# A two-layer decoder trunk on one core: affine halves behind the projection's low weights, the attention scale in the queries, later gate transposes, four up weights on the first token half

## The chip, the cores and the metric

One core of one Trainium2 chip runs the whole program in one launch. The metric is the device time of that launch in microseconds (us); the runs shown are three timed runs and one profiled execution of the kernel before.

## What is computed

The reference is a decoder trunk of two layers over 512 tokens of width 1024, in float32. Cut to what matters here, one layer is:

```python
proj = h @ w_in[l]                      # cq, ckv, kr, xp, xqk, xv, xo, ipre, fpre
a = mla(...)      # q = rms_norm(cq) @ w_uq ; k, v from ckv ; 4 heads, 128 + 64 (rotary)
                  # scale = (128 + 64) ** -0.5
                  # p = softmax(((q_nope * scale) . k_nope + (q_pe * scale) . k_pe) masked)
p = multiscale_pool(xp, ...)
m = mlstm(xqk, xv, xo, ipre, fpre, ...)  # gates give log weights, chunkwise matrix memory
h = layer_norm(ALPHA * h + concat(a, p, m) @ w_out[l])
x, g = split(h @ w_up[l])                # 2 x 2816 columns
h = layer_norm(ALPHA * h + (silu(dwconv(g)) * x) @ w_down[l])
```

A layer norm ends in an affine step, times a gain, plus a bias.

## The kernel before

Every float32 product is made of three products of shorter numbers: each operand x is split into `hi = round(x)` and `lo = x - hi`, and `hi*hi`, `hi*lo` and `lo*hi` are added in PSUM. For weights, `fetch` (L142) does this: SP loads 128x1024 floats into a `raw` buffer (two of them, `raw_...`), ACT casts them to `hi_...` (L158), and DVE, or for a few POOL, subtracts to get `lo_...` (L159). There are four `hi` and four `lo` buffers, used in turn, so a weight can be prepared only when the one four places before it has been used. The names of the weights: `ia`, `it`, `ib` (input projection), `uq`, `uk`, `uv`, `o{half}_{q}` (output projection, two halves of 512 columns, four chunks of 256 rows each; a trace row calls all of them `lo_o`), `up` and `d` (the MLP).

**Order of the work.** PE's instructions stand in the order in which a small planner in the program, `Order`, emits them: generators yield a cost, a delay, or the name of an event that they wait for, and the planner moves its own clock by them. The other engines' instructions are put in order by a scheduler from priorities and estimates when the program is built. Each engine runs its own list strictly in order; what it needs from another engine it waits for.

**Gates.** `mlstm` (L575 on) takes the forget gates to four rows of 512, makes two scans over them on DVE, and exponentiates the row `mr` on ACT (L597). After a delay of 10.0 in the planner (L598), PE turns `lf_r` and `mr` into columns by eight small transpositions into `cols` (L601, L602). Then come `mq` and `mk`, two block-diagonal products for each half j of the convolved channels `c[j]` (L616), and later the scores `st`. Between these, PE works on the input projection's chunks `ib`.

**Attention.** `att_scores` (L770 on) makes a block of scores `s_`, takes its row maximum `mx` on DVE (L791), multiplies it by -SCALE (L792), and ACT forms `exp(SCALE*s + mx)` with its row sum `sm` (L795). DVE takes the reciprocal (L796) and multiplies (L797); PE transposes the result (`pt`, L814).

**Output projection and norm.** `out_gen(0)` and `out_gen(1)` make the two halves. `h` is the residual stream, reloaded from the DRAM tile `spill` in four tiles of 128 tokens (L894); it was stored without its affine step, so `pre_affine(i, half)` multiplies 128x512 of it by the gain (L898) and adds the bias (L899), both on DVE. Then `resid` adds the product (L842) and takes statistics (L193). For `half == 0`, each `resid` also emits `pre_affine(i, 1)`, the affine step of the other half. In the second half, all tokens pass chunk 0 first; then, per token tile i, chunks 1, 2 and 3. `ln_tail` finishes a tile's norm: aggregate (L202), `rs` (L189, and a power on POOL, L190), normalise (L217). PE then transposes the tile (`tp_a`, L228) for the up projection.

**Up projection.** `t_half` makes its first products with 256 tokens (token tiles 0 and 1) for three weights, `up_0_0`, `up_0_1` and `up_1_0`, and then again for tiles 2 and 3 (L325); `t_one` makes the others with all 512 (L173 to L175).

Of the kernel before, what the change touches and what calls it, by code (L numbers as in the profile page):

```python
# [10 lines left out]
F32 = mybir.dt.float32  # L11
F32R = mybir.dt.float32r
BF16 = mybir.dt.bfloat16
AF = mybir.ActivationFunctionType
# [6 lines left out]
NT = S // P  # L21
# [74 lines left out]
def trunk(ctx: ExitStack, tc: tile.TileContext, I: dict, out: bass.AP, layers=DEPTH):  # L96
# [41 lines left out]
    wloaded = []  # L138
    first_raw = []

    def add_w(src, n, name, eng, rows=1):
        wlist.append((src, n, name, eng, rows))  # L142

    def fetch():
        src, n, name, eng, rows = wlist[len(wloaded)]
        if len(wloaded) < len(first_raw):
            raw = first_raw[len(wloaded)][:, :n]
        else:
            raw = stream.tile([P, CH], F32, tag="raw", bufs=2, name="raw_" + name)[:, :n]
        nc.sync.dma_start(raw, src)  # L150
        hi = stream.tile([P, CH], F32R, tag="whi", bufs=4, name="hi_" + name)
        lo = stream.tile([P, CH], F32R, tag="wlo", bufs=4, name="lo_" + name)
        if rows == 1:
            h_, l_, r_ = hi[:, :n], lo[:, :n], raw
        else:
            h_, l_ = [t.rearrange("p (r c) -> p r c", r=rows)[:, :, : n // rows] for t in (hi, lo)]
            r_ = raw.rearrange("p (r c) -> p r c", r=rows)
        A.copy(h_, r_)  # L158
        eng.tensor_tensor(l_, r_, h_.bitcast(F32), ALU.subtract)  # L159
        wloaded.append((hi, lo, name))  # L160
# [281 lines left out]
    for l in range(layers):  # L442
# [130 lines left out]
        def mlstm():  # L573
# [23 lines left out]
            A.activation(mr, mr, AF.Exp, scale=-1.0)  # L597
            yield 0.6, 10.0, None  # L598
            cols = bank("cols")
# [134 lines left out]
        def q_handler(base):  # L734
            def f(m, o):
                t = base + m
                if t < 4:
                    qn[t] = t4r(f"qn{t}")
                    split(*qn[t], o)
                    sch.set(f"qn{l}_{t}", 1.79)  # L740
# [32 lines left out]
        def att_scores():  # L773
            for hd in range(H):
# [4 lines left out]
                for qt in range(NT):  # L779
# [10 lines left out]
                    mx = small.tile([P, 1], F32, tag="mx", bufs=4, name="mx")  # L790
                    V.reduce_max(mx, s_[:, :n], AX.X)  # L791
                    V.tensor_single_scalar(mx, mx, -SCALE, ALU.mult)  # L792
                    p = pr[:, roff[qt] : roff[qt] + n]
                    sm = small.tile([P, 1], F32, tag="sm", bufs=4, name="sm")
                    A.activation(p, s_[:, :n], AF.Exp, bias=mx[:, 0:1], scale=SCALE, accum_out=sm)  # L795
                    V.reciprocal(sm, sm)  # L796
# [36 lines left out]
        def resid(which, nm, half, stt, cols=None, tail=True, dst=None):  # L833
            def f(i, ps):
# [4 lines left out]
                with ExitStack() as hs:  # L839
# [3 lines left out]
                    ln_stats(h, i, half, stt[i])  # L843
                if half == 0 and which == "g1":
                    hbox["pre"](i, 1)
                if half == 1:
# [61 lines left out]
        def ffn_open():  # L908
# [3 lines left out]
            fbox["lo"] = fa.tile([P, NF, S], F32R, name="f_lo")  # L912

        hold = {}
        f_sub = [None]
# [19 lines left out]
        def ffn_main():  # L935
            yield from until(o0)
            yield from until(out_gen(1))
            ffn_open()
            hbox["g1"] = load_gb(hp, I["ln1_g"][l], I["ln1_b"][l], "1")
            for k in range(NT):  # L940
                sch.add(ln_affine(h, k, hbox["g1"], f"f{l}_{2 + 2 * k}", lambda: f_sub[0]), 0)
            w1 = [[f"hT_a{l}_{i}" for i in range(2 * hf, 2 * hf + 2)] for hf in range(2)]
            yield from consume(t_half([f"up{l}_0_0", f"up{l}_0_1", f"up{l}_1_0"], w1),
                               lambda n, o: up_consume(n // 2, n % 2, o))
            for n in range(3, 2 * NF):
                yield from consume(t_one(f"up{l}_{n // 2}_{n % 2}"), lambda _, o, n=n: up_consume(n // 2, n % 2, o))
# [78 lines left out]
def tables():  # L1025
    inv = (1.0 / (np.float32(10000.0) ** (np.arange(0, ROPE, 2, dtype=np.float32) / np.float32(ROPE)))).astype(np.float32)
    ang = (np.arange(S, dtype=np.float32)[:, None] * inv[None, :]).astype(np.float32)
    cos, sin = np.cos(ang).astype(np.float32).T, np.sin(ang).astype(np.float32).T
    cs = np.zeros((P, 2, S), np.float32)
    for b in range(0, P, 64):  # L1030
        cs[b : b + 32, 0], cs[b + 32 : b + 64, 0] = cos, cos
        cs[b : b + 32, 1], cs[b + 32 : b + 64, 1] = sin, -sin
    icnt = np.zeros((P, 2, 16), np.float32)
# [24 lines left out]
```

## Time and profile before

| | |
|---|---|
| three timed runs | 1177.37, 1179.7, 1181.1 us (median 1179.7) |
| the profiled execution | 1175.83 us |
| its span, first to last instruction | 1174.0 us |
| mean granted clock of TensorE | 0.992 of full speed |
| PE busy | 1142.0 us, 97% of the span |
| DVE busy | 626.9 us, 53% |
| ACT busy | 469.0 us, 40% |
| POOL busy | 225.3 us, 19% |

PE is busy nearly all the time, so the time of the program is the work on PE plus the stretches in which PE waits or runs at the lower of its two clocks. The sum of a prediction is made against the profiled execution's own 1175.83 us.

### The profile page before, as it was taken

How to read it: one execution, taken by the hardware profiler on the slowest of the kernel's cores; microseconds unless marked ns; L12 is line 12 of the kernel's file. 1: busy time of each engine (PE TensorE's matmuls, PEld its weight loads, DVE VectorE, ACT ScalarE, POOL GpSimd, SP SyncE). 2: the span in 40 equal slices, each digit the busy share in tenths (PEclk: the TensorE clock that was granted, in tenths of full speed). 3: DMA queues.
4: the chain of work that ended last, by engine and by line, in shares of the span. 5: the costliest groups of instructions: out<-in, count | busy, mean ns of one | idle time of the engine just before them, and what ended most of it. 6: DMA issues, size and time to landing. Idle time of an engine off the chain costs nothing. (4 is left out here: it accounts for less than half of the span.)

```text
span 1174.0 us, 14137 instructions
## 1 busy us (share of the span) xinstructions
PE 1142.0 (97%) x5447; PEld 948.4 (81%) x5447; DVE 626.9 (53%) x1007; ACT 469.0 (40%) x814; POOL 225.3 (19%) x186
## 2 busy tenths in 40 slices
PE   8999999899999999999999999989999999999997
PEld 5878777788888888888886887868888888888885
DVE  6776986744453343223368569666544443432426
ACT  6573552553333333212266545417433433332110
POOL 0316400015331111000003362000333211110001
PEclk9999999999999999999999999989999999999999
DMA  8331213332332233233343212142333433233321
GB/s 293 104 117 48 85 37 143 127 107 90 105 128 97 101 91 107 90 93 105 102 138 125 64 48 92 45 171 73 115 102 103 130 93 105 90 99 99 91 89 72
DMA packets 34931, 120.77 MB, mean 103 GB/s; under 512 B 4392, under 2 KB 4904, under 8 KB 34864
## 3 DMA queue, kind: packets, MB, share of 16 engines
q1 hardware_dynamic: 34720, 119.61, 31.1%
q8 instruction: 43, 0.70, 0.2%
q10 hardware_dynamic: 144, 0.26, 0.1%
q14 instruction: 24, 0.20, 0.1%
HBM read 113.55 MB, written 6.31 MB: 102 GB/s over the span
## 5 line engine op out<-in xcount | busy, mean ns | idle before, releaser
L173 PE MATMUL t_up<-a_hi,hi_up 128*128 128x512 f32 x656 | 255.2, 389 | 0.0
L174 PE MATMUL t_up<-a_lo,hi_up 128*128 128x512 f32 x656 | 255.2, 389 | 0.0
L175 PE MATMUL t_up<-a_hi,lo_up 128*128 128x512 f32 x656 | 255.2, 389 | 0.0
L159 DVE TENSOR_TENSOR lo_up<-raw_up,hi_up 128x1024 fp32r<-128x1024 f32 x88 | 120.6, 1371 | 154.4 <-ACT hi_up L158 151.3
L158 ACT CAST hi_up<-raw_up 128x1024 fp32r<-128x1024 f32 x88 | 92.7, 1054 | 193.5 <-PE t_up L174 164.1
L930 POOL TENSOR_TENSOR f_lo<-y,f_hi 128x512 fp32r<-128x512 f32 x44 | 77.3, 1757 | 366.7 <-ACT f_hi L929 351.5
L173 PEld LDWEIGHTS t_up<-a_hi,hi_up 128*128 128x128 f32 x656 | 123.1, 188 | 25.6
L175 PEld LDWEIGHTS t_up<-a_hi,lo_up 128*128 128x128 f32 x656 | 123.1, 188 | 25.5
L174 PEld LDWEIGHTS t_up<-a_lo,hi_up 128*128 128x128 f32 x656 | 123.1, 188 | 25.5
L159 DVE TENSOR_TENSOR lo_d<-raw_d,hi_d 128x1024 fp32r<-128x1024 f32 x44 | 53.9, 1224 | 159.6 <-ACT hi_d L158 159.2
L290 PE MATMUL d<-hi_d,f_hi 128*128 128x512 f32 x352 | 137.1, 389 | 0.0
L292 PE MATMUL d<-hi_d,f_lo 128*128 128x512 f32 x352 | 136.9, 389 | 0.0
L291 PE MATMUL d<-lo_d,f_hi 128*128 128x512 f32 x352 | 136.9, 389 | 0.0
L158 ACT CAST hi_d<-raw_d 128x1024 fp32r<-128x1024 f32 x44 | 46.4, 1055 | 176.2 <-PE d L292 157.1
L292 PEld LDWEIGHTS d<-hi_d,f_lo 128*128 128x128 f32 x352 | 66.1, 188 | 13.8
L290 PEld LDWEIGHTS d<-hi_d,f_hi 128*128 128x128 f32 x352 | 66.1, 188 | 13.6
L291 PEld LDWEIGHTS d<-lo_d,f_hi 128*128 128x128 f32 x352 | 66.1, 188 | 13.6
L928 DVE TENSOR_TENSOR y<-y,t_up 128x512 f32<-128x512 f32 x44 | 30.3, 688 | 75.2 <-PE t_up L175 67.4
L923 DVE SCALAR_TENSOR_TENSOR y<-t_up,pp,y 128x511 f32<-128x511 f32 x88 | 65.7, 746 | 8.9 <-ACT y L921 7.3
L924 ACT ACTIVATE y<-y 128x512 f32<-128x512 f32 x44 | 27.8, 632 | 98.2 <-DVE y L923 98.0
L291 PE MATMUL o<-lo_o,a_hi 128*128 128x512 f32 x128 | 51.8, 405 | 8.6 <-DVE lo_o L159 8.6
L190 POOL TENSOR_TENSOR rs_d<-rs_d,nhalf 128x1 f32<-128x1 f32 x8 | 7.7, 968 | 234.9 <-DVE rs_d L189 234.9
(273 smaller groups left out, 1959.6 us busy)
## 6 DMA issues: line engine op xcount, KB each, us to landing
raw_up<-in_w_up_dram SPq DMA_DIRECT2D x88, 512.0 KB, 3.5
raw_d<-in_w_dn_dram SPq DMA_DIRECT2D x44, 512.0 KB, 3.5
raw_o<-in_w_out_dram SPq DMA_DIRECT2D x16, 512.0 KB, 3.5
raw_it<-in_w_it_dram SPq DMA_DIRECT2D x12, 512.0 KB, 3.5
spill<-h SPq DMA_DIRECT2D x8, 512.0 KB, 2.8
raw_ib<-in_w_ib_dram SPq DMA_DIRECT2D x8, 512.0 KB, 3.5
h<-spill SPq DMA_DIRECT2D x8, 512.0 KB, 7.9
raw_uq<-in_w_uq_dram SPq DMA_DIRECT2D x6, 384.0 KB, 2.9
```

The lines of the kernel that those rows point to most:

```text
L158: A.copy(h_, r_)
L159: eng.tensor_tensor(l_, r_, h_.bitcast(F32), ALU.subtract)
L173: T.matmul(o, whi, xhi, start=start, stop=False)
L174: T.matmul(o, whi, xlo, start=False, stop=False)
L175: T.matmul(o, wlo, xhi, start=False, stop=stop)
L290: T.matmul(o, xhi, whi, start=at == 0, stop=False)
L291: T.matmul(o, xhi, wlo, start=False, stop=False)
L292: T.matmul(o, xlo, whi, start=False, stop=at == nk - 1)
L923: V.scalar_tensor_tensor(y[:, t:], o[:, : S - t], w(2 - t), y[:, t:], ALU.mult, ALU.add)
L924: A.activation(y, y, AF.Silu)
L928: V.tensor_mul(y, y, o)
L930: f_sub[0] = G.tensor_sub(fbox["lo"][:, f, :], y, fbox["hi"][:, f, :].bitcast(F32)).ins
```

## The change

1. The affine steps of the second halves are no longer emitted by `resid`. `ffn_main` now emits them one by one during the second half's last group, with an order that puts each behind the subtraction that makes `lo_o1_3`, the projection's last low weight.
2. SCALE is folded into the queries (`qn` by a scaled copy and one scalar_tensor_tensor; the rotary part by scaled tables), so the multiplication of `mx` goes, and `reduce_max` gives the negated maximum.
3. The planner's delay ahead of the gate transposes is 13.0 in place of 10.0.
4. `t_half` takes four up weights on the first token half in place of three.

```diff
+    lo_ins = {}
...
-        eng.tensor_tensor(l_, r_, h_.bitcast(F32), ALU.subtract)
+        lo_ins[name] = eng.tensor_tensor(l_, r_, h_.bitcast(F32), ALU.subtract).ins
...
             A.activation(mr, mr, AF.Exp, scale=-1.0)
-            yield 0.6, 10.0, None
+            yield 0.6, 13.0, None
...
-                    split(*qn[t], o)
+                    A.mul(qn[t][0], o, SCALE)
+                    V.scalar_tensor_tensor(qn[t][1], o, SCALE, qn[t][0].bitcast(F32), ALU.mult, ALU.subtract)
...
-                    V.reduce_max(mx, s_[:, :n], AX.X)
-                    V.tensor_single_scalar(mx, mx, -SCALE, ALU.mult)
+                    V.reduce_max(mx, s_[:, :n], AX.X, negate=True)
...
-                    A.activation(p, s_[:, :n], AF.Exp, bias=mx[:, 0:1], scale=SCALE, accum_out=sm)
+                    A.activation(p, s_[:, :n], AF.Exp, bias=mx[:, 0:1], accum_out=sm)
...
-                if half == 0 and which == "g1":
-                    hbox["pre"](i, 1)
...
+        pre_left = list(range(NT))
...
             yield from until(o0)
-            yield from until(out_gen(1))
+            for y in out_gen(1):
+                if y[0] == "grp":
+                    last_grp = y[1] > 0
+                    continue
+                yield y
+                if last_grp and y[0] > 0 and pre_left:
+                    with tc.issue_after(lo_ins[f"o{l}_1_3"]):
+                        hbox["pre"](pre_left.pop(0), 1)
...
-            yield from consume(t_half([f"up{l}_0_0", f"up{l}_0_1", f"up{l}_1_0"], w1),
+            yield from consume(t_half([f"up{l}_0_0", f"up{l}_0_1", f"up{l}_1_0", f"up{l}_1_1"], w1),
                                lambda n, o: up_consume(n // 2, n % 2, o))
-            for n in range(3, 2 * NF):
+            for n in range(4, 2 * NF):
...
+    qcos, qsin = cos * np.float32(SCALE), sin * np.float32(SCALE)
     for b in range(0, P, 64):
-        cs[b : b + 32, 0], cs[b + 32 : b + 64, 0] = cos, cos
-        cs[b : b + 32, 1], cs[b + 32 : b + 64, 1] = sin, -sin
+        cs[b : b + 32, 0], cs[b + 32 : b + 64, 0] = qcos, qcos
+        cs[b : b + 32, 1], cs[b + 32 : b + 64, 1] = qsin, -qsin
```

The diff does not tell where the instructions come to stand. Three places follow, each from the list of one engine. First DVE of the kernel before, from the last affine steps to the normalisation of token tile 0 (`gb_p` holds gain and bias, `o_0` is the projection of tile 0, `st_a`, `mv_a` and `rs_a` its statistics):

```order
L899 TENSOR_TENSOR h_1967<-h_1967,gb_p 128x512
L842 SCALAR_TENSOR_TENSOR h_1967<-h_1967,o_3_1718 128x512
L898 TENSOR_TENSOR h_1967<-h_1967,gb_p 128x512
L193 BN_STATS st_a_2028<-h_1967 128x6
L899 TENSOR_TENSOR h_1967<-h_1967,gb_p 128x512
L159 TENSOR_TENSOR lo_o_1_2_2070<-raw_o_1_2_2067,hi_o_1_2_2069 128x1024
L159 TENSOR_TENSOR lo_o_1_3_2076<-raw_o_1_3_2073,hi_o_1_3_2075 128x1024
L842 SCALAR_TENSOR_TENSOR h_1967<-h_1967,o_0_2033 128x512
L193 BN_STATS st_a_1995<-h_1967 128x6
L202 BN_AGGR mv_a_2105<-st_a_1995 128x2
L189 TENSOR_SCALAR rs_a_2106<-mv_a_2105 128x1
L217 TENSOR_SCALAR h_1967<-h_1967,mv_a_2105,rs_a_2106 128x1024
```

All sixteen affine instructions, with four residual additions and four statistics, stand ahead of both low weights; behind them only tile 0's own five instructions lead to its normalisation.

DVE of the changed kernel, the same stretch: the low weight `lo_o_1_2` now stands behind two affine instructions.

```order
L160 TENSOR_TENSOR lo_o_1_1_2016<-raw_o_1_1_2013,hi_o_1_1_2015 128x1024
L897 TENSOR_TENSOR h_1951<-h_1951,gb_p 128x512
L898 TENSOR_TENSOR h_1951<-h_1951,gb_p 128x512
L160 TENSOR_TENSOR lo_o_1_2_2046<-raw_o_1_2_2043,hi_o_1_2_2045 128x1024
L897 TENSOR_TENSOR h_1951<-h_1951,gb_p 128x512
L843 SCALAR_TENSOR_TENSOR h_1951<-h_1951,o_0_1703 128x512
```

After it come the other first-half instructions (six affine, four residual, three statistics), then `lo_o_1_3`, one statistic, and this:

```order
L160 TENSOR_TENSOR lo_up_0_0_2058<-raw_up_0_0_2055,hi_up_0_0_2057 128x1024
L897 TENSOR_TENSOR h_1951<-h_1951,gb_p 128x512 x2
L898 TENSOR_TENSOR h_1951<-h_1951,gb_p 128x512 x2
L843 SCALAR_TENSOR_TENSOR h_1951<-h_1951,o_0_2009 128x512
L897 TENSOR_TENSOR h_1951<-h_1951,gb_p 128x512
L194 BN_STATS st_a_1979<-h_1951 128x6
L898 TENSOR_TENSOR h_1951<-h_1951,gb_p 128x512
L203 BN_AGGR mv_a_2087<-st_a_1979 128x2
L897 TENSOR_TENSOR h_1951<-h_1951,gb_p 128x512
L190 TENSOR_SCALAR rs_a_2088<-mv_a_2087 128x1
L898 TENSOR_TENSOR h_1951<-h_1951,gb_p 128x512
L218 TENSOR_SCALAR h_1951<-h_1951,mv_a_2087,rs_a_2088 128x1024
```

The eight affine instructions of the second halves now stand ahead of tile 0's normalisation, four of them in between its own steps.

PE at the gate transposes, before:

```order
L292 MATMUL ib_634<-hi_ib_0_594,a_lo 128x512
L601 MATMUL cols<-ident,lf_r 128x4
L602 MATMUL cols<-ident,mr 128x4
L601 MATMUL cols<-ident,lf_r 128x4
L602 MATMUL cols<-ident,mr 128x4
L601 MATMUL cols<-ident,lf_r 128x4
L602 MATMUL cols<-ident,mr 128x4
L601 MATMUL cols<-ident,lf_r 128x4
L602 MATMUL cols<-ident,mr 128x4
L616 MATMUL mq<-c,wbd 128x512
L616 MATMUL mk<-c,wbd 128x512
L290 MATMUL ib_631<-hi_ib_1_637,a_hi 128x512
```

And in the changed kernel:

```order
L293 MATMUL ib_632<-hi_ib_1_637,a_lo 128x512
L602 MATMUL cols<-ident,lf_r 128x4
L603 MATMUL cols<-ident,mr 128x4
L602 MATMUL cols<-ident,lf_r 128x4
L603 MATMUL cols<-ident,mr 128x4
L602 MATMUL cols<-ident,lf_r 128x4
L603 MATMUL cols<-ident,mr 128x4
L602 MATMUL cols<-ident,lf_r 128x4
L603 MATMUL cols<-ident,mr 128x4
L617 MATMUL mq<-c,wbd 128x512
L617 MATMUL mk<-c,wbd 128x512
L617 MATMUL mq<-c,wbd 128x512
```

The first twelve products of chunk `ib_1` now stand ahead of the transposes, and both pairs of `mq` and `mk` follow them at once; before, six `ib` products stood between the pairs. On PE there is one more move: `up_1_1` is made of 48 products of 256 columns in place of 24 of 512. The transposes of token tile 3 stay where they were, behind 36 of the 256-column products. On SP, the two loads of the next gain and bias (`gb`) now stand behind the loads of `raw_up_0_1` and `raw_up_1_0`. POOL's list is unchanged.

## Rows read from the trace of the kernel before

**Rows 1.** Waits of PE: waiting line, releaser, total us, times, longest us.

```profile
PE o L291 <- DVE lo_o L159: 8.6, 2, 5.1
PE cols L602 <- ACT mr L597: 3.6, 2, 2.0
PE pt L814 <- DVE pr L797: 2.9, 2, 1.5
PE tp_a L228 <- DVE h L217: 2.2, 2, 1.1
PE pt L814 <- DVE mx L792: 1.6, 2, 0.8
```

**Rows 2.** Timeline of PE, output projection's second half: start, us, instruction, [idle before, releaser].

```profile
203.72 0.39 PE L292 MATMUL o<-hi_o,a_lo 128*128 128x512 f32 x1
203.95 0.39 PE L290 MATMUL o<-hi_o,a_hi 128*128 128x512 f32 x1
207.81 0.50 PE L291 MATMUL o<-lo_o,a_hi 128*128 128x512 f32 x1 [3.48 <-DVE lo_o L159]
...
216.16 1.04 PE L228 MATMUL tp_a<-ident,h 128*128 128x128 f32 x8
...
783.78 0.80 PE L291 MATMUL o<-lo_o,a_hi 128*128 128x512 f32 x1 [5.10 <-DVE lo_o L159]
...
793.03 1.04 PE L228 MATMUL tp_a<-ident,h 128*128 128x128 f32 x8
```

**Rows 3.** Stretches: start:end, length, busy us of each engine, PEclk (granted clock), DMA share, GB/s.

```profile
59.00:63.00 4.00, 3.22 (x15) 2.11 (x16) 3.14 (x6) 2.24 (x4) 1.10 (x3) 1.00 0.46 165
636.00:639.00 3.00, 3.00 (x5) 1.34 (x4) 2.29 (x4) 1.98 (x4) 0.00 (x0) 0.50 0.50 195
155.00:157.00 2.00, 2.00 (x12) 1.91 (x11) 2.00 (x9) 0.64 (x3) 0.00 (x0) 0.50 0.00 0
730.00:734.00 4.00, 4.00 (x31) 3.44 (x30) 4.00 (x15) 2.75 (x10) 0.00 (x0) 1.00 0.07 30
209.00:212.00 3.00, 3.00 (x9) 2.35 (x8) 0.01 (x1) 0.00 (x0) 0.00 (x0) 0.50 0.69 239
783.00:789.00 6.00, 5.21 (x12) 4.13 (x13) 1.98 (x3) 1.05 (x1) 0.00 (x0) 0.50 0.80 306
```

**Rows 4.** Timeline of DVE, affine steps, low weights and tile 0's normalisation.

```profile
192.13 1.29 DVE L898 TENSOR_TENSOR h<-h,gb_p 128x512 f32<-128x512 f32 x2 [3.31 <-DMA h<-spill]
...
206.54 2.35 DVE L159 TENSOR_TENSOR lo_o<-raw_o,hi_o 128x1024 fp32r<-128x1024 f32 x2
...
214.50 0.81 DVE L217 TENSOR_SCALAR h<-h,mv_a,rs_a 128x1024 f32<-128x1024 f32 x1 [0.66 <-POOL rs_a L190]
...
768.11 1.29 DVE L898 TENSOR_TENSOR h<-h,gb_p 128x512 f32<-128x512 f32 x2 [4.94 <-DMA h<-spill]
```

**Rows 5.** Timeline of PE at the gate transposes, both layers.

```profile
59.78 0.22 PE L602 MATMUL cols<-ident,mr 4*128 4x4 f32 x1 [1.57 <-ACT mr L597]
...
66.62 0.40 PE L290 MATMUL ib<-hi_ib,a_hi 128*128 128x512 f32 x1
...
634.56 0.22 PE L602 MATMUL cols<-ident,mr 4*128 4x4 f32 x1 [1.99 <-ACT mr L597]
...
643.08 0.39 PE L290 MATMUL ib<-hi_ib,a_hi 128*128 128x512 f32 x1
```

**Rows 6.** Timeline of DVE, the last step of c[1] in layer 0.

```profile
62.51 0.69 DVE L518 TENSOR_TENSOR c<-c,th 128x512 f32<-128x512 f32 x1
```

**Rows 7.** Timeline of DVE at the first attention scores of layer 0.

```profile
149.33 1.22 DVE L159 TENSOR_TENSOR lo_o<-raw_o,hi_o 128x1024 fp32r<-128x1024 f32 x1
150.46 0.15 DVE L792 TENSOR_SCALAR mx<-mx 128x1 f32<-128x1 f32 x1
```

**Rows 8.** Timeline of PE, up projection on the first token half.

```profile
227.45 0.64 PE L325 MATMUL t_up<-a_hi,lo_up 128*128 128x256 f32 x4
227.93 0.64 PE L325 MATMUL t_up<-a_lo,hi_up 128*128 128x256 f32 x4
```

## The prediction

> **What bounds the kernel now.** I read the profile page first, then the waits of PE, then the timelines of PE and DVE around each wait, and last the granted clock of the same stretches. PE is busy for 97% of the span, so only two things can be won: time in which PE waits, and time in which it runs at half its clock. The waits [rows 1] name four places, each met once per layer: a low weight of the output projection (8.6 us in two waits), the gate transposes (3.6), the first attention transposes (2.9 + 1.6) and the last token tile's normalisation (2.2). That is 18.9 us. To the waits belongs what follows them: after several of them the granted clock is 0.50, the lower level (1.2 of 2.4 GHz) [rows 3], and a product of 512 columns takes twice its usual 0.23 us [rows 2].
>
> **The change, part by part.** The profiled execution is 1175.83 us; it lies 3.9 below the median of the timed runs.
>
> *Affine halves.* Before, DVE begins the affine steps when h has landed (192.13) and reaches the low weight at 206.54 [rows 4]: 14.4 us for 24 instructions, 0.60 each. PE begins the first product that uses this weight's chunk at 203.95 and waits for the low part until 207.81; in layer 1 it waits until 783.78 [rows 2]. After the change two affine instructions stand ahead of `lo_o_1_2`, so it starts at about 192.13 + 0.7 + 0.6 = 193.4 and is done at 194.7 (1.22 as in [rows 7]). `lo_o_1_3` stands 13 instructions further on: 194.6 + 13 x 0.60 = 202.4, done at 203.6; PE needs it at 203.95 + 7 x 0.23 = 205.6. Both are in time, and both waits go. In layer 1 everything on DVE is later by 768.11 - 192.13 = 575.98, and `lo_o_1_3` is done at 779.6; PE (idle from 783.78 - 5.10 = 778.7, when its product of 0.39 us had ended, which so began at 778.3) needs it at 779.9. That margin is only 0.3 us.
>
> What is late next is the normalisation of token tile 0, since the eight affine instructions of the second halves now stand ahead of it. From `lo_o_1_3` on, DVE has one statistic (0.6), `lo_up_0_0` (1.1) and four affine instructions (2.4) before tile 0's residual addition: 203.5 + 4.1 = 207.6. Then come addition, affine, statistic, affine, aggregate, affine, rs and affine, 0.6 each but for the two small ones: 211.5, and the normalisation with its 0.81 [rows 4] ends at 212.5. PE reaches `tp_a` after 30 products, 203.95 + 30 x 0.228 = 210.8, and waits 1.7. It begins `tp_a` at 212.5 in place of 216.16 [rows 2]: 3.6 won. In layer 1 the normalisation ends at 788.4, PE is there at 778.3 + 6.8 = 785.1 and waits 3.4; 788.5 in place of 793.03 is 4.5 won. A wait of 3.48 was followed by a half-clock stretch that took 1.75 (207.81 to 216.16 is 8.35 for 29 products of 0.228) and one of 5.10 by a stretch that took 2.65 (793.03 - 783.78 = 9.25) [rows 2, 3]. I charge the new 3.4 with 1.7 and the new 1.7 with nothing, since a wait of 1.57 left the clock at 1.00 [rows 3, 5]. Part 1 gives 3.6 + 4.5 - 1.7 = 6.4. Its bounds: 13.3 if tile 0 were no wait at all (PE at 210.8 and 785.1), 3.7 if both new waits cost a stretch as long as the old ones (8.1 - 1.75 - 2.65).
>
> *Gate transposes.* PE's order now has twelve 512-column products, 2.73 us, ahead of them. `mr` came 1.57 and 1.99 after PE wanted it [rows 5], so it is there first, by 1.0 us or less. In layer 0, from the idle's begin (59.78 - 1.57 = 58.21) to the 13th `ib` product (66.62) are 8.41 us, of which 6.84 are work at full clock [rows 3, 5]; the same work in layer 1 takes 643.08 - 632.57 = 10.51, as half of it ran at 0.50. Both losses go: 1.57 + 3.67 = 5.2. Taken back is a small new wait: both pairs of `mq` and `mk` are now adjacent, the second needs c[1] at 63.20 [rows 6], and PE is there at about 60.6 + 2.3 = 62.9. 0.3 in layer 0, between nothing and 0.3 in layer 1; part 3 gives 4.9. The scores move behind twelve more products and find their operands earlier, not later, than before.
>
> *Scale in the queries.* The 32 small multiplications (0.15 each [rows 7]) lie beside PE work but for the first two blocks of each layer. There the multiplication stands behind a weight subtraction of 1.22 that started right after the maximum was known [rows 7]. Now ACT can start on the maximum while DVE subtracts, so at 150.55 the first reciprocal can follow at once; what goes from the chain to the first transposition is one multiplication with its turn and the exponential that waited for it, about 0.7 us in each layer. The second wait shifts with the first and is not won twice. Of 4.5 us in four waits I take 1.4. In layer 0 these waits were followed by a stretch at 0.50, in layer 1 by none [rows 3]; with the waits at about 0.85 I take the stretch as gone, at the price 1.7 of the comparable one in [rows 2, 3]. Part 2 gives 3.1; bounds 0 and 4.5 + 1.7 = 6.2. A scaled copy and a scalar_tensor_tensor in place of a copy and a subtraction on 128x512 cost nothing that PE sees: they are as long, and their consumers come many products later.
>
> *Four up weights.* Tile 3's transposes stay behind the same 36 products, so their 1.1 us wait stays in each layer [rows 1]. Added is that 24 products of 512 columns (0.23 each [rows 2]) become 48 of 256 (0.48 for four [rows 8]): 5.76 - 5.52 = 0.24 in each layer, 0.5 in all. What they cover, the second half's operands, was not awaited by PE before. All four weight buffers are now held until the first weight's second half is done, but the next weight is wanted only 72 products, 8.6 us, later, and needs a cast and a subtraction.
>
> By TensorE: Matmul & The Clock Gate, section Back-to-back issue gap, a warm product takes N/2.4 ns plus 2.5 ns at N columns; halving the columns would then cost only 48 x 109.2 - 24 x 215.8 ns = 0.06 us in each layer, by the Trainium skill's formula, an estimate. The rows above say four times that, and the rows go into the sum.
>
> *The moved gain and bias loads* wait for the last affine step; the load behind them on SP needs a raw buffer that is freed later still. Nothing.
>
> **Sum:** 6.4 + 4.9 + 3.1 - 0.5 = 13.9. On the profiled execution that is 1175.83 - 13.9 = 1161.9; on the median of runs, which I forecast, 1179.7 - 13.9 = **1165.8**.
>
> **The rivals.**
>
> *Every leftover wait brings the lower clock.* Waits remain at tile 0 (1.7 and 3.4) and in attention. For it: 1.99 us brought a stretch in layer 1 [rows 3, 5]. Against it: 1.57 did not, nor did the attention waits of layer 1. Price: 1.75 at tile 0 in layer 0, 2.65 in place of 1.7 in layer 1, 1.7 in both attentions: 6.1 less, 1171.9. The Trainium skill speaks for it (TensorE: Matmul & The Clock Gate, section Part 1: The HAM clock gate): the lower clock is the default that recent activity lifts, and where it falls varies from run to run. The rows agree as far as they go, with a fall after one wait and none after a like one. Chance 0.15.
>
> *DVE is slower at tile 0.* If each of the 21 instructions after `lo_o_1_2` pays the 0.12 us that I allowed only where one needs its predecessor, tile 0 is 2.5 later in each layer: 1170.8. For it: the chains alternate on one h. Against: 24 such instructions took 0.60 each [rows 4]. Chance 0.09.
>
> *The timed runs hold more half-clock stretches than the profiled one*, and these go with their waits. Then the 3.9 us go too: 1161.9. For it: the two layers of one execution already differ. Against: 3.9 can lie outside the span. Chance 0.22.
>
> *Slower.* The four held buffers make the next up weight late. It decides if that weight's load, cast and subtraction take over 8.6 us from the release, and the time is over 1179.7 by 0.3% only if they take 8.6 + (13.9 + 3.5) / 2 = 17.3. For it: all four slots are full. Against: its raw buffer is free earlier, and a subtraction is 1.22. At 18 us it would be 1184.6. Chance 0.02.
>
> *It does not do what it says.* PE's and DVE's orders are as described, so only the transposes' wait for c[1] could replace that for `mr`; at 3 us per layer, part 3 gives nothing: 1170.7. Chance 0.04.
>
> **How the numbers follow.** Forecast 0.48. The range reaches from below the third rival to the first: 1158 to 1172. A measurement of this kernel can tell 0.3% (3.5 us) from no change; all cases but the slow one and half-realised mixtures pass it: faster 0.93, same 0.05, slower 0.02.
>
> **What would show it.** In the profile after: no wait of `o` for `lo_o`; `tp_a` waiting for h once per layer at tile 0 (1.7 and 3.4) and 1.1 at tile 3; no wait of `cols` for `mr`, at most 0.3 of `mq`; `pt` waits of about 0.85 each; 0.50 in the clock at most after layer 1's tile 0. The forecast is wrong if `tp_a` waits over 4 us in both layers, or if a wait at the up weights appears.

## The result, and the profile after

| | before | after |
|---|---|---|
| timed runs, median of four each | 1179.07 us | 1164.42 us (1162.76 to 1165.65) |
| profiled execution, its span | 1175.83, 1174.0 us | 1162.76, 1161.0 us |
| granted clock, mean | 0.992 | 0.997 |
| ratio of the timed runs, after to before | | 0.9874, 95% interval 0.9853 to 0.9896 |

The change made the kernel 14.65 us faster in the medians and 13.0 us faster in the two profiled spans. The forecast of 1165.8 us is 1.4 us off the median, and the range of 1158 to 1172 us holds it.

The busy times of the page after, then the waits of PE (waiting line, releaser, total us, times, longest us), which answer to [rows 1]:

```profile
PE 1138.9 (98%) x5495; PEld 947.4 (82%) x5495; DVE 624.4 (54%) x975; ACT 469.5 (40%) x814; POOL 226.5 (20%) x186
...
PE tp_a L229 <- DVE h L218: 6.7, 4, 2.3
PE pt L815 <- DVE pr L798: 3.0, 4, 0.8
```

Two rows of [rows 1] are gone: `o` for `lo_o` and `cols` for `mr`. The attention row for `mx` went too, and the one for `pr` now holds four shorter waits. The waits of `tp_a` for h rose from 2.2 to 6.7 us. Where they stand is told by the timeline of PE (start, us, instruction, [idle before, releaser]); its first two rows are the first head's probabilities in layer 0, the next two tile 0 and tile 3 of layer 0, the last two tile 0 and tile 3 of layer 1:

```profile
150.13 0.30 PE L815 MATMUL pt<-ident,pr 128*128 128x128 f32 x1 [0.80 <-DVE pr L798]
151.12 0.41 PE L815 MATMUL pt<-ident,pr 128*128 128x128 f32 x2 [0.69 <-DVE pr L798]
...
210.06 1.09 PE L229 MATMUL tp_a<-ident,h 128*128 128x128 f32 x8 [2.09 <-DVE h L218]
226.55 1.09 PE L229 MATMUL tp_a<-ident,h 128*128 128x128 f32 x8 [1.13 <-DVE h L218]
...
779.63 0.55 PE L229 MATMUL tp_a<-ident,h 128*128 128x128 f32 x3 [2.32 <-DVE h L218]
796.12 1.09 PE L229 MATMUL tp_a<-ident,h 128*128 128x128 f32 x8 [1.12 <-DVE h L218]
```

The gain is located by one PE instruction at each border of a stage: its start before less its start after. The difference between two borders is what that stage gave. Each row of the table is one such instruction; the starts come from the two timelines, of which six lines of layer 1 stand here (first `ib`, first `s` and first product of chunk 1, before and then after):

```profile
626.82 0.39 PE L290 MATMUL ib<-hi_ib,a_hi 128*128 128x512 f32 x1
720.15 0.28 PE L173 MATMUL s<-kn,qn 128*128 128x256 f32 x1
776.94 0.39 PE L290 MATMUL o<-hi_o,a_hi 128*128 128x512 f32 x1
...
621.12 0.39 PE L291 MATMUL ib<-hi_ib,a_hi 128*128 128x512 f32 x1
711.17 0.28 PE L174 MATMUL s<-kn,qn 128*128 128x256 f32 x1
768.99 0.39 PE L291 MATMUL o<-hi_o,a_hi 128*128 128x512 f32 x1
```

| border | layer 0: before, after, lead | layer 1: before, after, lead |
|---|---|---|
| first product of the input projection's `ib` | 52.46, 52.42, 0.04 | 626.82, 621.12, 5.70 |
| first product of the attention scores `s` | 144.24, 143.07, 1.17 | 720.15, 711.17, 8.98 |
| projection, second half, first product of chunk 1 | 202.59, 199.64, 2.95 | 776.94, 768.99, 7.95 |
| first transpose `tp_a` | 216.16, 210.06, 6.10 | 793.03, 779.63, 13.40 |
| first `d` product | 469.53, 463.81, 5.72 | 1046.40, 1033.39, 13.01 |

So the stage with the gates gave 1.17 - 0.04 = 1.1 us in layer 0 and 8.98 - 5.70 = 3.3 in layer 1. The attention gave 2.95 - 1.17 = 1.8 and then 7.95 - 8.98 = -1.0. The projection's end gave 3.15 and 5.45, and the up projection took 0.4 back in each layer.

A stretch at a granted clock of 0.50 is called a low stretch from here on. The clock around the places that are left (start:end, length, busy of each engine, granted clock, DMA share, GB/s), first where layer 1's attention begins, then from tile 0's wait on in both layers:

```profile
722.00:724.00 2.00, 2.00 (x12) 1.91 (x11) 2.00 (x6) 1.15 (x3) 0.00 (x0) 0.50 0.00 0
...
207.00:214.00 7.00, 4.91 (x27) 3.87 (x26) 5.67 (x12) 3.20 (x9) 1.54 (x2) 1.00 0.45 150
...
776.00:786.00 10.00, 7.68 (x42) 6.27 (x41) 7.73 (x16) 4.73 (x12) 1.55 (x2) 1.00 0.42 107
```

Of the four low stretches of [rows 3] none is left in its place, but a new one stands in the attention of layer 1, where [rows 3] had 1.00. Behind tile 0's waits of 2.09 and 2.32 us the clock stayed at 1.00.

The chain on DVE that [rows 4] led to, in layer 0: the affine start, the two low weights `lo_o_1_2` and `lo_o_1_3`, and tile 0's normalisation.

```profile
189.34 0.69 DVE L897 TENSOR_TENSOR h<-h,gb_p 128x512 f32<-128x512 f32 x1 [3.46 <-DMA h<-spill]
190.68 1.22 DVE L160 TENSOR_TENSOR lo_o<-raw_o,hi_o 128x1024 fp32r<-128x1024 f32 x1
...
199.59 1.22 DVE L160 TENSOR_TENSOR lo_o<-raw_o,hi_o 128x1024 fp32r<-128x1024 f32 x1
...
209.19 0.81 DVE L218 TENSOR_SCALAR h<-h,mv_a,rs_a 128x1024 f32<-128x1024 f32 x1 [0.44 <-POOL rs_a L191]
```

The whole stage stands 192.13 - 189.34 = 2.79 us earlier. With that taken off, the prediction had these starts at 190.6, 199.6 and 208.9.

### The profile page after: what moved, and what is told of

Same layout as the page of the kernel before. It is cut to its first block, busy times and chain, and to the rows that moved or that the text cites. A ratio compares the mean times of both kernels' runs of the same rounds, so it can differ in the third digit from the quotient of the medians.

```text
span 1161.0 us, 14179 instructions
## 1 busy us (share of the span) xinstructions
PE 1138.9 (98%) x5495; PEld 947.4 (82%) x5495; DVE 624.4 (54%) x975; ACT 469.5 (40%) x814; POOL 226.5 (20%) x186
## 5 line engine op out<-in xcount | busy, mean ns | idle before, releaser
L174 PE MATMUL t_up<-a_hi,hi_up 128*128 128x512 f32 x640 | 249.0, 389 | 0.0
L175 PE MATMUL t_up<-a_lo,hi_up 128*128 128x512 f32 x640 | 249.0, 389 | 0.0
L176 PE MATMUL t_up<-a_hi,lo_up 128*128 128x512 f32 x640 | 249.0, 389 | 0.0
L176 PEld LDWEIGHTS t_up<-a_hi,lo_up 128*128 128x128 f32 x640 | 120.1, 188 | 25.1
L174 PEld LDWEIGHTS t_up<-a_hi,hi_up 128*128 128x128 f32 x640 | 120.1, 188 | 25.0
L175 PEld LDWEIGHTS t_up<-a_lo,hi_up 128*128 128x128 f32 x640 | 120.1, 188 | 24.6
L291 PE MATMUL o<-hi_o,a_hi 128*128 128x512 f32 x128 | 50.9, 397 | 0.0
```

The costliest lines, as they stand in the source:

```text
L174: T.matmul(o, whi, xhi, start=start, stop=False)
L175: T.matmul(o, whi, xlo, start=False, stop=False)
L176: T.matmul(o, wlo, xhi, start=False, stop=stop)
L291: T.matmul(o, xhi, whi, start=at == 0, stop=False)
```

## The experiments

The theory was that the four parts add, each being worth the wait that it removes and the lower clock behind it, and that VectorE's order causes the waits that are left. The rivals were that the clock as a whole made the gain, or that VectorE's work is only put off. Four kernels undo one part of the change each, one is the changed kernel once more, and six go on from it. The kernels that were timed together had the kernel before beside them, with medians of 1176.68, 1176.97 and 1176.62 us in the three groups.

### The affine halves put back

```diff
+                if half == 0 and which == "g1":
+                    hbox["pre"](i, 1)
...
-                if last_grp and y[0] > 0 and pre_left:
-                    with tc.issue_after(lo_ins[f"o{l}_1_3"]):
-                        hbox["pre"](pre_left.pop(0), 1)
```

> The changed kernel with the second affine halves put back between the residual steps, so that they stand ahead of the last low weights on VectorE. Theory (the parts add, each is worth the wait that it removes): the two waits of the output projection for lo_o come back, 3.5 us in layer 0 and 5.1 us in layer 1, with a lower clock behind them, and the new waits of token tile 0's transposes for h (2.09 and 2.32 us) go; the profiled time rises by 7.5 to 9.5 us over the changed kernel's 1162.8 us, to 1170 to 1172 us, and some 0.6% of the ratio is gone. Rival (the gain of the change comes from the clock as a whole: five stretches of lower clock became one, and any part could have done that): the waits come back at the same size but without the 6.8 us stretch of half clock in layer 1, and the time rises by at most 5 us.

Measured: 1171.36 us median, span 1168.8 us, ratio to the kernel before 0.9955 (0.9939 to 0.997). The waits of PE and the two stretches behind them:

```profile
PE o L292 <- DVE lo_o L160: 7.2, 2, 3.8
...
PE tp_a L229 <- DVE h L218: 2.2, 2, 1.1
```

```profile
207.00:211.00 4.00, 4.00 (x12) 3.09 (x11) 0.89 (x3) 0.52 (x1) 0.00 (x0) 0.57 0.89 324
777.00:784.00 7.00, 6.11 (x14) 4.84 (x15) 2.94 (x4) 1.04 (x1) 0.00 (x0) 0.51 0.82 298
```

Between chunk 1 and `tp_a` the kernel lost 3.2 us against the changed one in layer 0 and 4.5 in layer 1, 7.6 in all. The waits alone are 7.2 - (6.7 - 2.2) = 2.7 of them; the rest is the lower clock behind the waits, which came back in both layers. The theory holds, and the rival, a rise of at most 5 us without the long low stretch in layer 1, does not. The wait in layer 1 was 3.77 us instead of the expected 5.1, and the low clock behind it was as long as in [rows 3]. In this execution the attention of layer 0 held a further stretch at the low clock and that of layer 1 none, which cost 1.2 us up to chunk 1 in the one and gave 1.3 in the other.

### The scale put back

```diff
-                    A.mul(qn[t][0], o, SCALE)
-                    V.scalar_tensor_tensor(qn[t][1], o, SCALE, qn[t][0].bitcast(F32), ALU.mult, ALU.subtract)
+                    split(*qn[t], o)
...
-                    V.reduce_max(mx, s_[:, :n], AX.X, negate=True)
+                    V.reduce_max(mx, s_[:, :n], AX.X)
+                    V.tensor_single_scalar(mx, mx, -SCALE, ALU.mult)
```

(with the exponential and the rotary tables to match)

> The changed kernel with the scale put back into the maximum and the exponential, so that VectorE has the 0.15 us multiplication between the scores and the softmax again. Theory of the prediction (two shorter waits per layer, 0.8 us each, and a half-clock stretch that the waits had brought): +3 us. Theory from the changed kernel's trace (the waits are 0.8 us shorter per layer, but the half-clock stretch did not go, it moved from the attention of layer 0 to that of layer 1, so the chip's clock there is not set by the length of these waits): +0.8 to +1.6 us, waits of pt of 1.5 and 0.8 us per layer again, and one half-clock stretch of 3.4 us in one of the two attentions. A stretch in both layers speaks for the first, in one or none for the second.

Measured: 1166.38 us median, span 1164.3 us, ratio 0.9918 (0.9898 to 0.9938).

```profile
151.45 0.30 PE L815 MATMUL pt<-ident,pr 128*128 128x128 f32 x1 [1.48 <-DVE pr L798]
152.57 0.41 PE L815 MATMUL pt<-ident,pr 128*128 128x128 f32 x2 [0.81 <-DVE mx L793]
```

```profile
718.00:724.00 6.00, 3.73 (x15) 2.49 (x14) 6.00 (x27) 4.01 (x15) 0.00 (x0) 0.76 0.61 175
781.00:785.00 4.00, 3.68 (x15) 3.06 (x16) 3.23 (x7) 2.93 (x9) 0.55 (x1) 0.69 0.91 253
```

From the first scores to the first value products the kernel lost 0.56 us in layer 0 and 0.46 in layer 1, with a low stretch in layer 1's attention in both kernels: in the profiles this part is worth 1.0 us. There the second theory holds. The rest of the 3.3 us in span is a low stretch behind tile 0's wait in layer 1 (0.69 above), where the changed kernel had 1.00 behind the same wait, and a begin of the program that was 0.5 us later. In the timed runs the part was worth more than 1.0: four of the six executions had a mean clock of 0.994, while the nine of the changed kernel lie between 0.995 and 0.998. So the lower clock may have come more often with the longer waits; one profile cannot show it.

### The gate transposes back

```diff
-            yield 0.6, 13.0, None
+            yield 0.6, 10.0, None
```

> The changed kernel with the delay of the gate transposes at 10.0 us instead of 13.0 us. Theory (each part is worth its own wait): the waits of the gate transposes for mr come back with 1.6 us in layer 0 and 2.0 us in layer 1, with a stretch of half clock of 3.4 us after the one in layer 1; +4 to +5 us, 1167 to 1168 us profiled. Rival (the half clock in layer 1's gates came from what stood ahead of it in the kernel before, the low clock of the output projection and of the stages before, and not from the wait): the waits come back, no half clock follows, and the time rises by 3 us or less.

Measured: 1167.88 us median, span 1167.8 us, ratio 0.993 (0.9908 to 0.9951).

```profile
60.52 0.22 PE L603 MATMUL cols<-ident,mr 4*128 4x4 f32 x1 [1.55 <-ACT mr L598]
...
632.15 0.22 PE L603 MATMUL cols<-ident,mr 4*128 4x4 f32 x1 [1.99 <-ACT mr L598]
```

```profile
632.00:636.00 4.00, 3.85 (x12) 2.08 (x12) 3.13 (x6) 2.24 (x4) 0.00 (x0) 0.57 0.53 173
212.00:216.00 4.00, 4.00 (x16) 3.32 (x15) 2.83 (x6) 3.45 (x10) 0.55 (x1) 0.59 0.65 222
786.00:790.00 4.00, 4.00 (x12) 3.09 (x12) 2.25 (x6) 3.67 (x10) 0.55 (x1) 0.57 0.54 153
```

The gate stages lost 1.1 and 3.3 us, 4.4 in all, just what the change had given there, and the low clock stands behind the wait of layer 1 again, although the stages ahead of it are those of the changed kernel. The theory holds. Here a low stretch followed tile 0's wait in both layers, 1.92 us in layer 0 and 2.27 in layer 1 (0.59 and 0.57 above), and neither attention had one.

### Three up weights on the first token half

```diff
-            yield from consume(t_half([f"up{l}_0_0", f"up{l}_0_1", f"up{l}_1_0", f"up{l}_1_1"], w1),
+            yield from consume(t_half([f"up{l}_0_0", f"up{l}_0_1", f"up{l}_1_0"], w1),
```

> The changed kernel with three up weights on the first token half instead of four. Theory (the fourth weight only costs, since two passes of 256 columns take 0.32 us per layer more than one of 512, and the wait of tile 3's transposes for h stands at 1.1 us with it and without it): -0.6 us, tile 3's wait still 1.1 us per layer. Rival (with the affine halves moved, the second token half's normalisations come late, and the fourth weight covers them): a wait of the up products for h or of the transposes for h of 2 us or more appears in the second half, and the time rises by 1 to 3 us.

Measured: 1164.46 us median, span 1162.2 us, ratio 0.9904 (0.9884 to 0.9923). From `tp_a` to `d` in layer 0 and from `t_up` to `d` in layer 1 the kernel gained 0.30 and 0.36 us, and tile 3's wait was 1.12 and 1.08 us. The two stages are 0.7 us shorter together, as the theory had it; in the timed runs this is too small to be told from nothing. The low clock fell in two other places than in the changed kernel:

```profile
151.00:155.00 4.00, 3.58 (x13) 2.66 (x14) 4.00 (x16) 2.90 (x12) 0.00 (x0) 0.64 0.49 174
718.00:724.00 6.00, 4.51 (x30) 3.44 (x30) 5.96 (x21) 4.18 (x16) 0.00 (x0) 1.00 0.54 175
779.00:783.00 4.00, 3.44 (x14) 2.95 (x15) 3.23 (x7) 2.69 (x8) 0.55 (x1) 0.65 0.90 245
```

### The changed kernel once more

> The changed kernel itself once more, to have it beside the others on one chip and to see where its stretches of half clock fall a second time. Theory (where they fall is a matter of the execution: the waits open the places, and not each place has one each time): the waits on TensorE are the same to 0.1 us, the stretches of 3.4 us at 0.50 stand in other places than the one in the attention of layer 1, and the profiled span lies within 3 us of 1161.0 us in steps of about 1.7 us. Rival (the program fixes them): again one stretch, in the attention of layer 1, and a span within 1 us.

Measured: 1164.14 us median (1162.65 to 1165.55), profiled span 1161.0 us, ratio 0.9889 (0.9873 to 0.9905).

```profile
719.00:724.00 5.00, 4.64 (x22) 3.89 (x23) 5.00 (x18) 3.76 (x14) 0.00 (x0) 0.69 0.36 119
```

My theory missed for the profiled execution: again one stretch, in the same place, and the same span. Its other four executions had spans of 1160.9 to 1163.7 us at mean clocks of 0.997 to 0.995, so their number of low stretches was probably not always one. The four kernels above have the same attention and tile-0 waits within 0.2 us where their edit does not touch them, but all save one of their low stretches there stand elsewhere: which of the like waits gets one can differ from kernel to kernel, with an edit far from it.

### Affine pairs by tile

```diff
+            norm_ins[0] = V.tensor_scalar(z, z, mv[:, 0:1], rs[:, 0:1], ALU.subtract, ALU.mult).ins
...
+                if last_grp and y[0] > 0:
+                    steps += 1
+                    if steps % 3 == 1:
+                        with tc.issue_after(norm_ins[0] if pre_left[0] else lo_ins[f"o{l}_1_3"]):
+                            hbox["pre"](pre_left.pop(0), 1)
```

> The changed kernel, but each tile's second affine pair stands on VectorE behind the normalisation of the tile before it, and only tile 0's right behind the low weights. Theory (tile 0's wait of 2.09 and 2.32 us is VectorE working off the affine pairs of later tiles before tile 0's normalisation): both waits fall under 0.5 us, 4 us are gained, 1158 to 1160 us. Rival (the work is only put off): the wait moves to tiles 1 to 3, whose transposes then wait 1 us or more each for h, and the time is the same within 1.5 us.

Measured: 1160.74 us median, span 1158.1 us, ratio 0.9863 (0.9845 to 0.988).

```profile
222.12 0.74 PE L327 MATMUL t_up<-a_lo,hi_up 128*128 128x256 f32 x4 [0.65 <-DVE a_lo L181]
226.06 1.09 PE L230 MATMUL tp_a<-ident,h 128*128 128x128 f32 x8 [1.76 <-DVE h L219]
```

Tile 0's wait is gone in both layers, and from the first value products to `tp_a` 2.2 us were gained in each. Of these 1.5 us were given back up to `d`: a wait for `a_lo` of 0.65 is new, and tile 3's grew from 1.13 to 1.76. So the rival was mostly right on the waits: 0.6 to 0.8 us per layer remain. On the time the theory was nearer: the span is 2.9 us shorter and the median 3.4, and the profiled execution's 1159.86 us lies in its 1158 to 1160. For 1.6 us of the 2.9 the reason is another: this execution did not have the low stretch of layer 1's attention, behind waits that are the same.

### The low parts on GpSimd

```diff
-                add_w(I["w_out"][l, half, q], 1024, f"o{l}_{half}_{q}", G if half == 0 and q < 2 else V)
+                add_w(I["w_out"][l, half, q], 1024, f"o{l}_{half}_{q}", G if half == 0 else V)
```

> The changed kernel with the low parts of the third and fourth weight of the projection's first half subtracted on GpSimd like those of the first and second, so that VectorE is free at the first scores. Theory (the waits of the first two transposes of the probabilities, 0.8 and 0.7 us per layer, come from the two subtractions of 1.22 us that stand ahead of the first maximum and reciprocal): these waits fall under 0.3 us in both layers, 2 to 3 us are gained, and no stretch of half clock falls in the attention. Rival (the first tile's softmax is as long as PE's wait by itself: maximum, exponential, reciprocal, multiplication, one after the other): the waits stay at 0.5 us or more, the time is the same within 1 us.

Measured: 1166.07 us median, span 1164.7 us, ratio 0.9903 (0.9887 to 0.9919), 1.9 us over the changed kernel's median beside it. Both expectations missed, but for the absence of a low stretch in the attention. Timelines ahead of layer 0's attention: two pairs of subtractions on DVE in the changed kernel, the same pairs here, and POOL and PE here:

```profile
142.05 1.41 DVE L731 TENSOR_TENSOR qp<-qp,qp 64x512 fp32r<-64x512 f32 x2
144.21 1.40 DVE L731 TENSOR_TENSOR qp<-qp,qp 64x512 fp32r<-64x512 f32 x2
```

```profile
143.76 3.50 DVE L731 TENSOR_TENSOR qp<-qp,qp 64x512 fp32r<-64x512 f32 x2
147.29 0.69 DVE L180 TENSOR_TENSOR v<-uv,v 128x512 fp32r<-128x512 f32 x1
148.01 2.76 DVE L731 TENSOR_TENSOR qp<-qp,qp 64x512 fp32r<-64x512 f32 x2
```

```profile
143.97 2.74 POOL L160 TENSOR_TENSOR lo_o<-raw_o,hi_o 128x1024 fp32r<-128x1024 f32 x1 [3.78 <-ACT hi_o L159]
...
146.96 2.55 POOL L160 TENSOR_TENSOR lo_o<-raw_o,hi_o 128x1024 fp32r<-128x1024 f32 x1
```

```profile
151.55 0.38 PE L174 MATMUL s<-kn,qn 128*128 128x256 f32 x1 [2.24 <-DVE v L180]
```

In the changed kernel the two pairs of `qp` subtractions took 1.41 and 1.40 us. Here they took 3.50 and 2.76. The first pair ended at 147.26, 0.55 us or one such subtraction after the one on POOL (143.97 + 2.74 = 146.71); the second at 150.77, 1.26 us or two of them after POOL's (149.51). The instruction on `v` between them, one of whose inputs is in PSUM, kept its 0.69. So the scores waited 2.24 us for DVE, more than the two waits of 0.8 and 0.7 that were to go, and of these one of 0.63 is still there. From the first scores to the first value products the stage took 15.6 us in both layers; the changed kernel took 14.1 in layer 0 and, with its low stretch, 15.7 in layer 1. So 1.5 us were lost where the changed kernel had no low stretch, and nothing was won where this one had none. The other 2.1 us of the longer span were lost near the program's start, with a low stretch there. The Trainium skill states such a rule (SBUF — State Buffer, section SBUF: two separate sides): a VectorE instruction with two SBUF inputs and a GpSimd instruction that reads SBUF share a port pair, and the one that comes second waits for the whole of the first. The rows agree with it.

### Both, and tile 3 later

```diff
-        yield 0.0, dve_free[0] + 0.72 - sch.now, None
+        yield 0.0, dve_free[0] + (2.04 if name[0] == "a" and i == NT - 1 else 0.72) - sch.now, None
```

> The two edits of the kernels by tile and with the low weights on GpSimd together, and token tile 3's transposes behind the second token half's first up products (planned 2.04 us after VectorE is free instead of 0.72 us). Theory (the waits add, and where no wait is left there is no stretch of half clock): all waits of tp_a for h and of pt for pr fall under 0.5 us, 9 us are gained against the changed kernel, 1152 to 1156 us, no stretch at half clock between 20 us and the end, and the eleven runs lie closer together than those of the changed kernel. Rival (the clock falls by itself from time to time, waits or not): the waits go, 9 us less those stretches, 2 to 4 of them per execution remain and the time stays at 1156 to 1160 us.

Measured: 1162.39 us median, span 1160.6 us, ratio 0.9875 (0.9857 to 0.9892). The 9 us did not come, since the part on GpSimd lost 1.5 us in the attention of layer 0 and 0.3 in that of layer 1, and a low stretch near the program's start, which the kernel with the low parts on GpSimd had too, cost 2 us. But with tile 3's transposes later its wait fell to 0.3 us, and from the first value products to `d` the two other edits gave 2.1 and 2.3 us. The rival, a clock that falls without waits, is not borne out: both low stretches stood right behind waits, of 0.9 us at the start and of 2.27 in layer 1's attention.

### Two edits, without GpSimd

This kernel has the affine pairs by tile and the later transposes of tile 3.

> The changed kernel with the affine pairs by tile and token tile 3's transposes behind more up products (planned 2.04 us after VectorE is free), without the subtractions on GpSimd. Theory (in the kernel with all three edits these two gave 2.1 and 2.3 us per layer between the start of the projection and the down products, and the subtractions on GpSimd took 1.4 us per layer back in the attention): 4.4 us are gained against the changed kernel, a span of 1156 to 1157 us with one stretch of half clock in the attention of layer 1, 1155 us without it. Rival (the wait for h at tile 3 went in that kernel because the whole stage stood later, by the GpSimd loss): tile 3's wait stays at 1.8 us, and the gain is under 2 us.

Measured: 1159.51 us median, span 1157.7 us, ratio 0.9853 (0.9831 to 0.9875).

```profile
226.63 1.09 PE L230 MATMUL tp_a<-ident,h 128*128 128x128 f32 x8 [0.33 <-DVE h L219]
...
794.32 1.09 PE L230 MATMUL tp_a<-ident,h 128*128 128x128 f32 x8 [0.32 <-DVE h L219]
```

From the first value products to `d` it gained 2.05 us in layer 0 and 2.2 in layer 1, with a low stretch in layer 1's attention as in the changed kernel. The theory holds; the span is 3.3 us shorter and not 4.4, as 0.8 us were lost ahead of the first attention.

### The low parts queued later on VectorE

```diff
+                    pr_ins[hd, qt] = V.tensor_scalar_mul(p, p, sm[:, 0:1]).ins
...
+        with ExitStack() as hs:
+            if name[0] == "o" and name[2:] in ("_0_2", "_0_3"):
+                hs.enter_context(tc.issue_after(pr_ins[0, 1]))
+            lo_ins[name] = eng.tensor_tensor(l_, r_, h_.bitcast(F32), ALU.subtract).ins
```

> The kernel with the two edits, and on VectorE the low parts of the projection's third and fourth weight queued behind the second multiplication of the first head's softmax instead of ahead of it. Theory (the two waits of 0.8 and 0.7 us at the first transposes of the probabilities are these two subtractions of 1.22 us, VectorE's work and not the length of the softmax): the waits fall under 0.4 us per layer, 2 to 3 us are gained over the kernel with two edits, a span of 1152 to 1154 us, and no stretch of half clock in the attention. Rival (VectorE is busy without a gap from 146 to 158 us, so its work is only put off): a wait of the same size appears behind, at the transposes of the larger tiles or at the products with the values, and the time is the same within 1 us.

Measured: 1155.61 us median (1155.3 to 1156.17), span 1154.4 us, ratio 0.9825 (0.9801 to 0.9849): the fastest kernel here. PE's wait in the attention, once per layer, and the clock of that place in layer 1 and of layer 1's projection end:

```profile
151.60 0.55 PE L820 MATMUL pt<-ident,pr 128*128 128x128 f32 x3 [0.86 <-DVE mx L798]
```

```profile
714.00:722.00 8.00, 7.14 (x49) 6.02 (x48) 7.93 (x25) 5.28 (x18) 0.00 (x0) 1.00 0.22 66
772.00:795.00 23.00, 22.03 (x147) 19.62 (x146) 18.40 (x31) 16.47 (x38) 1.64 (x3) 1.00 0.31 93
```

Both waits of 0.8 and 0.7 went and one of 0.86 came behind them, so both sides were half right: against the kernel with the two edits the stage gained 0.9 us per layer. In layer 1 another 1.55 us came from the clock, and in layer 0 0.6 us were given back ahead of `d`, with a new wait of 0.52 for a low weight. No low stretch was left up to PE's last product, the five executions had mean clocks of 0.998 or 0.999, and they lie within 0.9 us of each other. In the kernel before, beside this one, spans went from 1169.2 us at a clock of 0.995 to 1177.3 us at 0.987.

### That kernel with three up weights

> The kernel with the low parts queued later, with three up weights on the first token half instead of four. Theory (the fourth weight costs 0.32 us per layer and is a cover only where tile 3's transposes would wait longer than that without it): with tile 3's transposes later than in the changed kernel the products of the three weights end about 5.8 us earlier than those of four, and since VectorE's chain has not become shorter a wait of 1 us or more per layer for h comes back; +1 to +4 us over the kernel with four. Rival (the fourth weight only costs): -0.6 us, no new wait.

Measured: 1158.73 us median, span 1156.9 us, ratio 0.9853 (0.983 to 0.9875).

```profile
230.51 0.74 PE L331 MATMUL t_up<-a_hi,hi_up 128*128 128x256 f32 x4 [1.77 <-ACT a_hi L184]
```

```profile
230.00:235.00 5.00, 4.49 (x25) 4.49 (x26) 1.39 (x2) 2.14 (x5) 0.00 (x0) 0.66 0.33 105
```

The wait came in layer 0 with a low stretch behind it, and from `tp_a` to `d` the kernel lost 2.1 us; in layer 1 it lost 0.5, with a wait of 0.26 where 1 or more was expected. The theory holds on the sum, 3.1 us in the medians, but not for layer 1. So the fourth weight costs 0.3 us per layer in the profiles while tile 3's transposes stand where the change has them, and is a cover once they stand later.

## Why the prediction was right

**Affine halves**, predicted +6.4, measured 3.15 + 5.45 = 8.6 in the profile and 7.6 when undone. The mechanism was as told: both waits of [rows 2] went, and tile 0 came next. The starts on DVE were within 0.3 us. For layer 0 the predicted wait was 1.7 and the measured one 2.09. For layer 1 it was 3.4 and 2.32, since h landed 9.2 us earlier (768.11 [rows 4] against 758.92) while PE came 7.95 earlier; the prediction had let DVE's delay to PE stand as it was before. The 1.7 charged for a low stretch behind that wait was not paid in this profile, but one came there in three others (scale, gates, three up weights). So layer 0 gave less than the predicted 3.6 and layer 1 more than 4.5 - 1.7 = 2.8, and the sum of the two was too small.

**Gate transposes**, predicted +4.9, measured 1.1 + 3.3 = 4.4, and 4.4 when undone. No wait of `mq` for `c[1]` came.

**Scale**, predicted +3.1, measured 1.8 - 1.0 = 0.8, and 1.0 when undone. In the profiles this is the term that was mis-sized. The step that failed there is "with the waits at about 0.85 I take the stretch as gone, at the price 1.7". The waits did become 0.80, 0.69, 0.82 and 0.68. But the stretch went in layer 0 and another came in layer 1 behind like waits, so nothing was won by it in this execution. The prediction also allowed a low clock only behind layer 1's tile 0, and the one that came stood here. The 1.4 us for the waits themselves was a little high: 1.0 came back when the part was undone. In the timed runs undoing it cost 2.5 us, which their noise cannot tell from 3.1 or from 1.0.

**Four up weights**, predicted -0.5, measured -0.8, and -0.7 when undone. The rows of [rows 8] had the right order of size; the estimate of 0.06 us per layer from the Trainium skill's formula (TensorE: Matmul & The Clock Gate, section Back-to-back issue gap) was too small, at 0.3 to 0.4 measured. In the timed runs the part is not told from nothing.

**The sum** was 13.9, and the profile says 13.0. Undone one by one, the parts are worth 7.6 + 4.4 + 1.0 - 0.7 = 12.3 there. In the medians, each against the kernel before of its group, the changed kernel is 12.8 us faster and the four are 5.3, 8.8, 10.3 and 12.2 faster, so the parts are worth 7.5, 4.0, 2.5 and 0.6, together 14.7, with some 3 us of uncertainty on each. So the parts add within what these runs can tell. Since the terms erred in both directions in the profile, part of the closeness is luck.

**The rivals.** The lower clock behind every leftover wait is half right: each of the attention and tile-0 places had a low stretch in the profile of the changed kernel or of one with a part undone, but no profile had one in all four places. A slower DVE at tile 0 did not come: the normalisation began at 209.19 against 208.9. More low stretches in the timed runs of before, gone with their waits, are not shown: the medians are 1.65 us further apart than the profiled spans in the first group, but 12.8 against 13.0 in the later one. The slower case and the one without effect did not come.

What stays open is why, of like waits, one brings the low clock and another doesn't. The thirteen profiles do show that the length of the wait alone does not decide. All 21 low stretches ahead of PE's last product stood in a wait of at least 0.68 us or right behind one. Waits of 3.4 us or more had one in 4 of 4 cases and tile 0's waits of 1.9 to 2.3 us in 4 of 12. The pair of about 0.8 and 0.7 us in the attention had one in 5 of 14, but tile 3's single waits of 1.1 us in none of 16. No experiment set the reason apart.

## What to carry to other kernels

When work is moved off the front of an engine's queue, the next thing that this queue feeds becomes the wait: cost it from the queue's order, and place each piece just behind the last consumer that is more urgent. Price a wait and the low clock behind it separately; for waits up to 2.3 us the second was here a chance per place and not a fixed sum, and waits of 0.8 and 0.7 us in a row could still bring it. A cover that only costs in one order of the work may be needed in the next, so test it again after each move.

## What was not expected of the hardware

Two subtractions moved to GpSimd held up VectorE: a pair of its instructions with two inputs in SBUF took 3.50 us instead of 1.41, while the neighbour with an input in PSUM kept its 0.69. And the spread of the timed runs was largest where the waits were longest: 8.1 us over nine spans of the kernel before in the last group, 0.9 us over five of the kernel whose longest wait after 25 us was 0.86 us.
